# A decoder trunk on one core: the operands' byte addresses, and 1/rms moved from up to down's results

## The chip, the core and the metric

The kernel runs on one of the eight cores of a Trainium2 chip. The metric is the device time of one execution in microseconds (us), as the median of several runs. A profile is one more execution, recorded instruction by instruction. The engines are PE (TensorE, which multiplies matrices; its weight loads are listed as PEld), DVE (VectorE), ACT (ScalarE), POOL (GpSimd) and SP, which here only issues DMAs. They run side by side, each through its own list of instructions in order, and wait for one another by semaphores.

## The reference

The input is a sequence of 512 tokens with 1024 features in float32. There are two layers, and in each one a feed-forward block (FFN), a mixer, and a second FFN, every one of them behind an RMS norm:

```
def rmsnorm(x, g):
    y = x * rsqrt(mean(x * x, axis=-1) + 1e-6)
    return y * g
def swiglu(h, w_gate, w_up, w_down):
    return (silu(h @ w_gate) * (h @ w_up)) @ w_down
x = x + 0.5 * swiglu(rmsnorm(x, g[0]), w_gate[i, 0], w_up[i, 0], w_down[i, 0])
x = x + mixer(rmsnorm(x, g[1]))     # layer 0: attention, layer 1: Mamba-2 SSD
x = x + 0.5 * swiglu(rmsnorm(x, g[2]), w_gate[i, 1], w_up[i, 1], w_down[i, 1])
...
return rmsnorm(x, final_norm)
```

The FFN's hidden width is 2816. The mixer of layer 0 is sliding-window and native sparse attention, that of layer 1 a Mamba-2 scan. The 1/rms of a norm is one number per token, so it can be multiplied in at any place before the next nonlinear step: before silu on the gate, and anywhere down to the result on the up branch.

## The kernel before

Activations lie transposed, features in the 128 partitions and the 512 tokens along the free dimension: `xT` is 8 pieces of 128x512, and `d` counts the pieces. To keep float32 accuracy with the faster float32r matmul, each operand is split into a rounded high part and the rest (`xh` and `xl`, `whi` and `wlo`), and `mm3` (L118 to L122) multiplies high by high, high by low and low by high into the same PSUM bank. A norm's gain is multiplied into `xh` and `xl` when they are made; the 1/rms (`rB`, a PSUM bank of 128x512) is not, and is multiplied into results.

An FFN (`ffn`, L1091) goes twice through the stages gate_up and down, each time with 11 of the 22 tiles of 128 hidden features. In gate_up each tile `f` needs the 128x512 results of gate and up. The first one or two tiles of an FFN are done plainly (`gate_up_direct`, with 512 columns to a matmul): two in the first FFN, one in the others. The other 83 tiles of the program use a Strassen-Winograd scheme (`gate_up`): seven products p1 to p7 with 256 columns each, 84 matmuls in all, whose weights are sums that POOL makes (`sa`, `sb`, L1166). The right-hand operands are the 8 slots of 256 columns in `xh` and `xl`. ACT casts the weights to `whi` (L95), DVE subtracts to get `wlo` (L96), and the two have three buffers each. DVE adds the products up to `gu` (four instructions of L1211), `scale_gu` multiplies gate and up, 1024 columns, by 1/rms (L1219), ACT takes silu of the gate (L1223), DVE multiplies by up (L1224), and `pair` (L240) splits the product to `ah` and `al`, the operands of down. Five PSUM banks (`bs`) serve the products, four of them to a tile.

In down each of the 8 pieces `d` is a sum over the 11 tiles, 33 matmuls with 512 columns on `ah` and `al`, into one of two banks (`bm`). `residual` (L1229) adds half of it to `xT`. In the second half of an FFN the piece then goes to the next norm (`norm_piece`). `last` (L1258) does the same for the very last piece in two halves of 256 columns, with the final norm behind it.

The mixers use `xh` and `xl` with 512 columns: 14 tiles of queries and keys in attention, 48 tiles of the SSM's input (`ssm_tiles`), 24 matmuls each. Later matmuls of attention read probabilities (`th`, `tl`, L548 to L551), those of the SSM's output read `yh` and `yl`.

`xh` and `xl` come from a pool that is filled from the right-hand end of SBUF, and that is opened anew for each norm (`open_x`, L141). In the built program they and the other operands start at these bytes of a partition:

| tile | byte | past a multiple of 128 |
|---|---|---|
| `xh`, `xl` in the FFNs | 163808, 196576 | 96 |
| `xh`, `xl` in the mixers | 196576, 212960 | 96 |
| `ah`, `al` | 78720, 101248 | 0 |
| `th`, `tl` in attention's second part | 195776 to 210112 | 64 |
| `yh`, `yl` | 95104 to 117632 | 0 |
| `whi`, `wlo` | 33664 to 54144 | 0 |

Slots and pieces are 1024 and 2048 bytes long, so every matmul on a tile has the tile's own offset. The order on each engine is not the code's: a scheduler that estimates durations sorts the instructions of every engine when the program is built.

Of the kernel before, what the change touches and what calls it, by code (L numbers as in the profile page):

```python
# [14 lines left out]
F32 = mybir.dt.float32  # L15
# [6 lines left out]
P = 128  # L22
# [18 lines left out]
class Trunk:  # L41
    def __init__(self, ctx, tc, aps):
        self.ctx, self.tc, self.nc, self.aps = ctx, tc, tc.nc, aps
        nc = self.nc
        self.cst = ctx.enter_context(tc.tile_pool(name="cst", bufs=1))
        self.wp = ctx.enter_context(tc.tile_pool(name="wp", bufs=3))
        self.rawp = ctx.enter_context(tc.tile_pool(name="rawp", bufs=2))
        self.one = ctx.enter_context(tc.tile_pool(name="one", bufs=1))
        self.xT = self.cst.tile([P, ND, T], F32, name="xT")
        self.xpool = None  # L50
        self.gains = self.cst.tile([P, 7, ND], F32, name="gains")
        nc.sync.dma_start(out=self.gains, in_=aps["gains"])
        self.epsc = self.cst.tile([P, 1], F32, name="epsc")
        nc.vector.memset(self.epsc, EPS)
        self.onesD = self.cst.tile([P, P], F32, name="onesD")
        nc.vector.memset(self.onesD, 1.0 / D)
        self.n = 0
        self.ahead = None
        nc.scalar.preload_act_table_set("natural_log_exp_and_others")
# [81 lines left out]
    def open_x(self):  # L141
# [9 lines left out]
        shape = [P, 4, 8, 256] if self.strassen else [P, ND, T]  # L151
        self.xh = pool.tile(shape, F32R, name=f"xh_{self.n}")
        self.xl = pool.tile(shape, F32R, name=f"xl_{self.n}")

    def close_x(self):
        if self.xpool is not None:
# [934 lines left out]
    def ffn(self, li, fi, nxt):  # L1091
        nc, tc = self.nc, self.tc
        with tc.tile_pool(name=f"a{li}{fi}", bufs=1, reuse_waits="tile") as ap, tc.tile_pool(
# [9 lines left out]
            for st in range(2):  # L1103
# [5 lines left out]
                for d in DORD:  # L1109
# [9 lines left out]
                            for f in range(k0, k0 + n):  # L1119
                                self.mm3(b, *w[f], ah[:, f], al[:, f], f == 0, f == HF - 1)  # L1120
                    if not end:
                        self.residual(d, b, 0.5, st == 1)
                if self.which == 6 and st == 1:
                    self.last(d, w, ah, al)

# [8 lines left out]
    def gate_up_direct(self, li, fi, f, ah, al):  # L1134
# [8 lines left out]
                self.mm3(b.rearrange("p (i t) -> p i t", i=2), hi[:, d], lo[:, d], *x, d == 0, d == 7)  # L1143
        if f == 0:
            self.late_operands()
        t = self.ft([P, 7, 256], "gu")
        g, u = (t[:, i : i + 2].rearrange("p i t -> p (i t)") for i in (1, 3))
        for out, b in zip((g, u), bs):
            nc.scalar.copy(out=out, in_=b)
        self.scale_gu(t)  # L1150
        self.activate(bs[0], g, u, ah, al)

    def gu_weights(self, li, fi, f, engine):

# [14 lines left out]
    def gate_up(self, li, fi, f, ah, al):  # L1169
# [35 lines left out]
        for out, x, y in (  # L1205
# [3 lines left out]
            (t[:, 2:4], t[:, 0:7:6], halves(bw)),  # L1209
        ):  # L1210
            nc.vector.tensor_tensor(out=out, in0=x, in1=y, op=ALU.add)  # L1211
        self.scale_gu(t)
        g, u = (t[:, i : i + 2].rearrange("p i t -> p (i t)") for i in (1, 3))
        self.activate(by, g, u, ah, al)

    def scale_gu(self, t):
        gu = t[:, 1:5].rearrange("p (m i) t -> p m (i t)", m=2)
        r = self.rB.unsqueeze(1).to_broadcast([P, 2, T])
        self.nc.vector.tensor_tensor(out=gu, in0=gu, in1=r, op=ALU.mult)  # L1219

    def activate(self, b, g, u, ah, al):

        self.nc.scalar.activation(out=b, in_=g, func=AF.Silu)  # L1223
        self.nc.vector.tensor_tensor(out=b, in0=u, in1=b, op=ALU.mult)  # L1224
        self.pair(ah, al, b)

    def residual(self, d, b, scale, last=True, acc=None, ts=slice(0, T)):
        x = self.xT[:, d, ts]
        self.nc.vector.scalar_tensor_tensor(  # L1229
            out=x, in0=b, scalar=scale, in1=x, op0=ALU.mult, op1=ALU.add  # L1230
        )
        if not last:
            return
        if self.which == 6:
            self.square_piece(self.xT[:, d])
        else:
            self.norm_piece(d, acc=acc, late=d % 4 == 3)
# [20 lines left out]
    def last(self, d, w, ah, al):  # L1258
# [9 lines left out]
        for ts, n in zip(halves, (4, 2)):  # L1268
            b = self.bank("m")[:, ts]
            for f in range(HF):  # L1270

                with self.tc.issue_after(mean) if ts.start and f > 3 else nullcontext():
                    self.mm3(b, *w[f], ah[:, f, ts], al[:, f, ts], f == 0, f == HF - 1)
            self.residual(d, b, 0.5, False, ts=ts)
            x = self.xT[:, d, ts]
            ms, r = self.bank("s")[:, ts], self.bank("s")[:, ts]
            sq, y, z = (self.t512(t)[:, ts] for t in ("s", "t1", "t2"))
# [115 lines left out]
```

## Time and profile before

| | us |
|---|---|
| median of 3 runs (2237.49 to 2240.22) | 2237.62 |
| the profiled execution's own time | 2238.98 |
| its span, first to last instruction | 2237.2 |
| PE busy in it | 2167.8 (97%) |
| DVE busy | 1675.6 (75%) |
| ACT busy | 1154.4 (52%) |
| POOL busy | 810.3 (36%) |

The time outside the span is 1.8 us. Matmuls are pipelined: one lasts some 0.28 us with 256 columns and 0.39 us with 512, while the next starts long before it has ended. So the rate of PE is read from starts, not from durations: the start of one matmul and that of a later one, divided by the number of matmuls between. A DVE instruction starts up to 0.08 us before the one in front of it has ended.

### The profile page before, as it was taken

The page shows a single profiled execution, that of the slowest core. Times are in us where ns is not written, and L with a number is a line of the kernel's source. Part 1 is how long each engine was busy: PE and PEld are TensorE (multiplying, and loading weights), DVE is VectorE, ACT ScalarE, POOL GpSimd, SP SyncE. Part 2 cuts the span into 40 slices and gives each one's busy share as a digit, 9 for nine tenths or more (in the row PEclk, how much of TensorE's full clock was granted, in tenths as well). Part 3 has the DMA queues.
Part 4 walks back from the last instruction along what each step waited for, and adds up shares of the span by engine and source line. Part 5 has one row for each costly group of instructions (what it writes and reads, how often), then busy time and mean ns, then how long its engine had stood idle before and what let it go on. Part 6 is the DMA issues. An engine that isn't in the chain of part 4 may idle for free.

```text
span 2237.2 us, 34473 instructions
## 1 busy us (share of the span) xinstructions
PE 2167.8 (97%) x13488; PEld 1935.3 (87%) x13488; DVE 1675.6 (75%) x2430; ACT 1154.4 (52%) x1814; POOL 810.3 (36%) x602
## 2 busy tenths in 40 slices
PE   8999999978999999999999999999999998999998
PEld 5999997867888998998998997788788877998997
DVE  6975984585788975986984984677667668984984
ACT  7533544445566533445542444677667666442543
POOL 1623621432013623622632630244344435622630
PEclk9999999989999999999999999999999999999999
DMA  3222335516302322232322233656565651232322
GB/s 132 95 97 102 107 104 147 133 48 152 76 2 66 114 97 102 96 103 96 112 97 102 95 109 106 172 142 151 118 157 142 160 143 57 104 103 96 114 97 83
DMA packets 48449, 242.04 MB, mean 108 GB/s; under 512 B 6624, under 2 KB 9696, under 8 KB 31136
## 3 DMA queue, kind: packets, MB, share of 16 engines
q1 hardware_dynamic: 36048, 195.28, 25.7%
q0 software_dynamic: 12240, 44.57, 10.5%
q8 instruction: 106, 1.74, 0.3%
q14 instruction: 55, 0.45, 0.1%
HBM read 193.04 MB, written 2.23 MB: 87 GB/s over the span
## 4 chain that ended last, share of the span: by engine, by line
PE 88%; DVE 6%; ACT 2%; DMA 1%; issue 1%; POOL 0%; DVEq 0%; SPq 0%; ACTq 0%; POOLq 0%
PE bm L120 14%; PE bm L122 13%; PE bm L121 13%; PE bs L120 13%; PE bs L122 13%; PE bs L121 13%; DMA wlo<-raw 1%; PE bt L536 1%; DVE xl L244 1%; PE bs L487 1%; DVE wlo L96 1%; PE bo L551 1%; PE bs L482 1%; PE bo L548 1%; PE bs L488 0%
## 5 line engine op out<-in xcount | busy, mean ns | idle before, releaser
L120 PE MATMUL bs<-xh,whi 128*128 128x256 f32 (+1 forms) x2404 | 684.5, 289 | 8.8 <-ACT whi L95 2.9
L121 PE MATMUL bs<-xl,whi 128*128 128x256 f32 (+1 forms) x2404 | 682.0, 286 | 4.1 <-DVE xl L244 4.1
L122 PE MATMUL bs<-xh,wlo 128*128 128x256 f32 (+1 forms) x2404 | 665.5, 287 | 4.5 <-DVE wlo L96 4.5
L95 ACT CAST whi<-raw 128x1024 fp32r<-128x1024 f32 (+3 forms) x312 | 256.8, 826 | 449.4 <-PE bm L121 221.7
L120 PEld LDWEIGHTS bs<-xh,whi 128*128 128x128 f32 x2404 | 452.0, 188 | 25.2 <-issue 9.6
L121 PEld LDWEIGHTS bs<-xl,whi 128*128 128x128 f32 x2404 | 453.4, 189 | 10.8 <-DVE xl L244 5.9
L122 PEld LDWEIGHTS bs<-xh,wlo 128*128 128x128 f32 x2404 | 444.1, 189 | 10.5 <-DVE wlo L96 5.8
L96 DVE TENSOR_TENSOR wlo<-raw,whi 128x1024 fp32r<-128x1024 f32 (+3 forms) x304 | 350.9, 1157 | 111.0 <-ACT whi L95 109.2
L1166 POOL TENSOR_TENSOR sa<-raw 128x512 f32<-128x512 f32 x82 | 111.8, 1364 | 674.2 <-DVE wlo L96 294.5
L121 PE MATMUL bm<-al,whi 128*128 128x512 f32 (+1 forms) x715 | 276.0, 386 | 0.0
L122 PE MATMUL bm<-ah,wlo 128*128 128x512 f32 (+1 forms) x715 | 275.8, 386 | 0.0
L120 PE MATMUL bm<-ah,whi 128*128 128x512 f32 (+1 forms) x715 | 274.8, 386 | 0.0
L109 POOL DMA_DIRECT2D wlo<-raw x85 | 73.6, 866 | 452.6 <-ACT wlo L108 447.2
L1229 DVE SCALAR_TENSOR_TENSOR xT<-bm,xT 128x512 f32<-128x512 f32 (+1 forms) x113 | 77.3, 685 | 165.3 <-PE bm L122 165.3
L122 PE MATMUL bm<-xh,wlo 128*128 128x512 f32 x488 | 195.4, 401 | 4.5 <-DMA wlo<-raw 4.5
L120 PE MATMUL bm<-xh,whi 128*128 128x512 f32 x488 | 195.9, 401 | 1.5 <-DVE xT L1229 0.9
L121 PE MATMUL bm<-xl,whi 128*128 128x512 f32 x488 | 194.5, 399 | 0.0
L1166 POOL TENSOR_TENSOR sa<-sa,raw 128x512 f32<-128x512 f32 x82 | 168.0, 2049 | 5.7
L122 PEld LDWEIGHTS bm<-ah,wlo 128*128 128x128 f32 x715 | 134.3, 188 | 27.1
L121 PEld LDWEIGHTS bm<-al,whi 128*128 128x128 f32 x715 | 134.3, 188 | 26.9
L120 PEld LDWEIGHTS bm<-ah,whi 128*128 128x128 f32 x715 | 134.3, 188 | 26.7
L96 DVE TENSOR_TENSOR wlo<-sb,whi 128x1024 fp32r<-128x1024 f32 x83 | 152.7, 1839 | 1.3 <-ACT whi L95 1.3
(397 smaller groups left out, 4245.2 us busy)
## 6 DMA issues: line engine op xcount, KB each, us to landing
raw<-wgu SPq DMA_DIRECT2D x88, 1024.0 KB
raw<-wdn SPq DMA_DIRECT2D x64, 704.0 KB
wlo<-raw POOLq DMA_DIRECT2D x85, 512.0 KB, 4.7
raw<-m_win SPq DMA_DIRECT2D x24, 1024.0 KB
raw<-m_wout SPq DMA_DIRECT2D x8, 1024.0 KB
raw<-wqk SPq DMA_DIRECT2D x6, 1024.0 KB
raw<-cw SPq DMA_DIRECT2D x4, 1024.0 KB
raw<-wo SPq DMA_DIRECT2D x4, 1024.0 KB
```

Of the source, the lines that this page charges most:

```text
L95: nc.scalar.copy(out=hi[:, :n], in_=raw)
L96: (lo_engine or nc.vector).tensor_tensor(out=lo[:, :n], in0=raw, in1=hi[:, :n].bitcast(F32), op=ALU.subtract)
L109: nc.gpsimd.dma_start(out=lo[:, :n], in_=raw, accum_op=ALU.add)
L120: nc.tensor.matmul(out, wh, xh, start=start, stop=False)
L121: nc.tensor.matmul(out, wh, xl, start=False, stop=False)
L122: nc.tensor.matmul(out, wl, xh, start=False, stop=stop)
L244: nc.vector.tensor_tensor(out=lo, in0=src, in1=hi.bitcast(F32), op=ALU.subtract)
L482: nc.tensor.matmul(s[j], q_hi, k_hi, start=True, stop=False)
L487: nc.tensor.matmul(s[j], q_hi, k_lo, start=False, stop=False)
L536: nc.tensor.transpose(t[:, at : at + P], p[:, j, k0 : k0 + P], self.idf)
L1166: engine.tensor_tensor(out=out, in0=x, in1=y, op=op)
L1229: self.nc.vector.scalar_tensor_tensor(out=x, in0=b, scalar=scale, in1=x, op0=ALU.mult, op1=ALU.add)
```

## The change

Two things change. First, a tile of 32 bytes (`edge`) is put at the right-hand end of SBUF, and in the mixers a tile of 64 bytes (`xe`) beside `xh` and `xl`. That moves the operands:

| tile | byte before | byte now | past a multiple of 128 now |
|---|---|---|---|
| `xh`, `xl` in the FFNs | 163808, 196576 | 163776, 196544 | 64 |
| `xh`, `xl` in the mixers | 196576, 212960 | 196480, 212864 | 0 |

Second, `scale_gu` is gone. The gate alone is multiplied by 1/rms, from `gu` into a PSUM bank (L1225 of the new kernel), and silu works in that bank. In the plain tiles gate is read from its bank without a copy. Up is left as it is; instead `residual` multiplies each result of down by 1/rms, in its bank (L1233), before it is added. For that an SBUF copy of 1/rms, `rF`, is made once for each FFN.

```
+        edge = ctx.enter_context(tc.tile_pool(name="edge", bufs=1, side="right"))
+        edge.tile([P, 8], F32, name="edge")
...
         self.xl = pool.tile(shape, F32R, name=f"xl_{self.n}")
+        if not self.strassen:
+            pool.tile([P, 16], F32, name=f"xe_{self.n}")
...
-                        self.residual(d, b, 0.5, st == 1)
+                        self.residual(d, b, 0.5, st == 1, r=self.rF)
...
-        t = self.ft([P, 7, 256], "gu")
-        g, u = (t[:, i : i + 2].rearrange("p i t -> p (i t)") for i in (1, 3))
-        for out, b in zip((g, u), bs):
-            nc.scalar.copy(out=out, in_=b)
-        self.scale_gu(t)
-        self.activate(bs[0], g, u, ah, al)
+        if f == 0:
+            r = self.rB
+            self.rF = self.ft([P, T], "rF", 1)
+            nc.scalar.copy(out=self.rF, in_=r)
+        u = self.ft([P, 7, 256], "gu")[:, 3:5].rearrange("p i t -> p (i t)")
+        nc.scalar.copy(out=u, in_=bs[1])
+        self.activate(bs[0], bs[0], self.rF, u, ah, al)
...
-        self.scale_gu(t)
         g, u = (t[:, i : i + 2].rearrange("p i t -> p (i t)") for i in (1, 3))
-        self.activate(by, g, u, ah, al)
-
-    def scale_gu(self, t):
-        gu = t[:, 1:5].rearrange("p (m i) t -> p m (i t)", m=2)
-        r = self.rB.unsqueeze(1).to_broadcast([P, 2, T])
-        self.nc.vector.tensor_tensor(out=gu, in0=gu, in1=r, op=ALU.mult)
-
-    def activate(self, b, g, u, ah, al):
-        self.nc.scalar.activation(out=b, in_=g, func=AF.Silu)
+        self.activate(by, g, self.r, u, ah, al)
+
+    def activate(self, b, g, r, u, ah, al):
+        self.nc.vector.tensor_tensor(out=b, in0=g, in1=r, op=ALU.mult)
+        self.nc.scalar.activation(out=b, in_=b, func=AF.Silu)
         self.nc.vector.tensor_tensor(out=b, in0=u, in1=b, op=ALU.mult)
         self.pair(ah, al, b)
 
-    def residual(self, d, b, scale, last=True, acc=None, ts=slice(0, T)):
+    def residual(self, d, b, scale, last=True, acc=None, ts=slice(0, T), r=None):
         x = self.xT[:, d, ts]
+        if r is not None:
+            self.nc.vector.tensor_tensor(out=b, in0=b, in1=r[:, ts], op=ALU.mult)
         self.nc.vector.scalar_tensor_tensor(
             out=x, in0=b, scalar=scale, in1=x, op0=ALU.mult, op1=ALU.add
         )
...
-            self.residual(d, b, 0.5, False, ts=ts)
+            self.residual(d, b, 0.5, False, ts=ts, r=self.rF)
```

The scheduler's order changes with it. The new file's lines stand 3 to 8 further down: L99 is the old L96, L1218 the old L1211, L1227 the old L1224, L249 the old L244. On DVE one tile of gate_up, in the second half of the first FFN, stood as follows (`wlo` belongs to the weights of the tile behind it, `al` to the tile in front).

```order
L1219 TENSOR_TENSOR gu_2692<-gu_2692,br_169 128x1024
L96 TENSOR_TENSOR wlo_2801<-raw_2704,whi_2800 128x512
L1224 TENSOR_TENSOR bs_2601<-gu_2692,bs_2601 128x512
L1211 TENSOR_TENSOR gu_2816<-e_2817,bs_2725 128x2x256
L96 TENSOR_TENSOR wlo_2837<-raw_2828,whi_2836 128x1024
L1211 TENSOR_TENSOR gu_2816<-gu_2816,bs_2726 128x256
L244 TENSOR_TENSOR al_88<-bs_2601,ah_87 128x512
L1211 TENSOR_TENSOR gu_2816<-gu_2816,bs_2724 128x2x256
L96 TENSOR_TENSOR wlo_2841<-sa_2830,whi_2840 128x1024
L1211 TENSOR_TENSOR gu_2816<-gu_2816,bs_2727 128x512
L96 TENSOR_TENSOR wlo_2845<-sb_2831,whi_2844 128x1024
```

The same tile on DVE now:

```order
L1225 TENSOR_TENSOR bs_2613<-gu_2704,br_173 128x512
L99 TENSOR_TENSOR wlo_2813<-raw_2716,whi_2812 128x512
L1227 TENSOR_TENSOR bs_2613<-gu_2704,bs_2613 128x512
L1218 TENSOR_TENSOR gu_2828<-e_2829,bs_2737 128x2x256
L249 TENSOR_TENSOR al_92<-bs_2613,ah_91 128x512
L99 TENSOR_TENSOR wlo_2849<-raw_2840,whi_2848 128x1024
L1218 TENSOR_TENSOR gu_2828<-gu_2828,bs_2738 128x256
L1218 TENSOR_TENSOR gu_2828<-gu_2828,bs_2736 128x2x256
L99 TENSOR_TENSOR wlo_2853<-sa_2842,whi_2852 128x1024
L1218 TENSOR_TENSOR gu_2828<-gu_2828,bs_2739 128x512
L99 TENSOR_TENSOR wlo_2857<-sb_2843,whi_2856 128x1024
```

The multiplication by 1/rms has 512 columns instead of 1024, and `al` has moved from behind the large `wlo<-raw` to the place in front of it. On ACT the same tile stood thus:

```order
L1223 ACTIVATE bs_2601<-gu_2692 128x512
L1204 COPY e_2817<-bs_2724 128x256
L95 CAST whi_2836<-raw_2828 128x1024
L243 CAST ah_87<-bs_2601 128x512
L95 CAST whi_2840<-sa_2830 128x1024
```

And on ACT it stands now (L98 is the old L95, L248 the old L243, L1211 the old L1204):

```order
L1226 ACTIVATE bs_2613<-bs_2613 128x512
L1211 COPY e_2829<-bs_2736 128x256
L248 CAST ah_91<-bs_2613 128x512
L98 CAST whi_2848<-raw_2840 128x1024
L98 CAST whi_2852<-sa_2842 128x1024
```

The cast to `ah` has passed the cast of the next weights to `whi`, as `al` did on DVE. In down of the same half, one piece on DVE was this:

```order
L1229 SCALAR_TENSOR_TENSOR xT<-bm_3355,xT 128x512
L96 TENSOR_TENSOR wlo_3459<-raw_3456,whi_3458 128x768
L223 TENSOR_TENSOR acc_3251<-acc_3251,t_364_3400 128x512
L168 SCALAR_TENSOR_TENSOR xl_3205<-xT,gains,xh_3204 128x512
L96 TENSOR_TENSOR wlo_3481<-raw_3456,whi_3480 128x640
```

And one piece is now:

```order
L1233 TENSOR_TENSOR bm_3371<-bm_3371,rF_288 128x512
L99 TENSOR_TENSOR wlo_3477<-raw_3474,whi_3476 128x768
L1234 SCALAR_TENSOR_TENSOR xT<-bm_3371,xT 128x512
L228 TENSOR_TENSOR acc_3265<-acc_3265,t_365_3417 128x512
L173 SCALAR_TENSOR_TENSOR xl_3217<-xT,gains,xh_3216 128x512
L99 TENSOR_TENSOR wlo_3499<-raw_3474,whi_3498 128x640
```

Each piece has one instruction of 512 columns more, and the first `wlo` stands between the two steps of the residual.

## Rows read from the trace of the kernel before

**Rows 1.** The page: busy time of the engines, and the chain by engine.

```profile
PE 2167.8 (97%) x13488; PEld 1935.3 (87%) x13488; DVE 1675.6 (75%) x2430; ACT 1154.4 (52%) x1814; POOL 810.3 (36%) x602
...
PE 88%; DVE 6%; ACT 2%; DMA 1%; issue 1%; POOL 0%; DVEq 0%; SPq 0%; ACTq 0%; POOLq 0%
```

**Rows 2.** Windows, length, engines' busy time, clock: early tile, late tile, start, down, stage.

```profile
219.08:229.16 10.08, 10.08 (x86) 10.08 (x85) 9.81 (x12) 5.16 (x7) 6.43 (x4) 1.00 0.30 105
280.41:290.80 10.39, 10.31 (x84) 10.13 (x85) 10.32 (x12) 5.07 (x8) 6.42 (x4) 1.00 0.30 100
44.00:58.00 14.00, 9.34 (x64) 7.89 (x63) 13.37 (x23) 9.12 (x15) 3.11 (x2) 1.00 0.22 75
333.00:340.50 7.50, 7.50 (x35) 6.22 (x34) 3.73 (x5) 2.81 (x4) 0.00 (x0) 1.00 0.28 97
198.80:311.30 112.50, 112.11 (x925) 111.14 (x924) 107.81 (x118) 54.56 (x75) 62.54 (x40) 1.00 0.29 98
```

**Rows 3.** Timeline: start us, length us, PE in gate_up, 84 matmuls apart.

```profile
753.39 0.28 PE L120 MATMUL bs<-xh,whi 128*128 128x256 f32 x1
...
763.47 0.28 PE L120 MATMUL bs<-xh,whi 128*128 128x256 f32 x1
```

**Rows 4.** Timeline of PE in down, 33 matmuls apart.

```profile
176.39 0.39 PE L120 MATMUL bm<-ah,whi 128*128 128x512 f32 x1
...
183.87 0.39 PE L120 MATMUL bm<-ah,whi 128*128 128x512 f32 x1
```

**Rows 5.** Timeline of PE in attention's input, 12 matmuls apart.

```profile
395.56 0.39 PE L120 MATMUL bm<-xh,whi 128*128 128x512 f32 x1
...
398.36 0.39 PE L120 MATMUL bm<-xh,whi 128*128 128x512 f32 x1
```

**Rows 6.** Timeline of PE in attention: pairs 4 and 7 matmuls apart.

```profile
591.08 0.28 PE L548 MATMUL bo<-th,vh 128*128 128x256 f32 x1
...
591.53 0.39 PE L551 MATMUL bo<-tl,vh 128*128 128x256 f32 x2
...
609.75 0.28 PE L548 MATMUL bo<-th,vh 128*128 128x256 f32 x1
...
610.58 0.28 PE L549 MATMUL bo<-th,vl 128*128 128x256 f32 x1
```

**Rows 7.** DVE by form in four late tiles: busy us, mean ns, idle before.

```profile
L96 DVE TENSOR_TENSOR wlo<-raw,whi 128x1024 fp32r<-128x1024 f32 x4 | 8.7, 2172 | 0.0
...
L96 DVE TENSOR_TENSOR wlo<-sa,whi 128x1024 fp32r<-128x1024 f32 x4 | 4.9, 1214 | 0.0
L1219 DVE TENSOR_TENSOR gu<-gu,br 128x1024 f32<-128x1024 f32 x4 | 4.8, 1207 | 0.0
...
L1224 DVE TENSOR_TENSOR bs<-gu,bs 128x512 f32<-128x512 f32 x4 | 2.8, 696 | 0.3
```

**Rows 8.** Timeline around the border of two late tiles.

```profile
279.87 0.41 DVE L1211 TENSOR_TENSOR gu<-gu,bs 128x256 f32<-128x256 f32 x1
...
280.06 0.28 PE L122 MATMUL bs<-xh,wlo 128*128 128x256 f32 x1
...
280.42 0.36 PE L120 MATMUL bs<-xh,whi 128*128 128x256 f32 x1
```

**Rows 9.** Timeline of DVE, ACT and POOL inside a late tile.

```profile
287.08 1.05 ACT L95 CAST whi<-raw 128x1024 fp32r<-128x1024 f32 x1
...
287.96 1.28 POOL L1166 TENSOR_TENSOR sb<-raw,sa 128x512 f32<-128x512 f32 x1
288.03 0.58 ACT L243 CAST ah<-bs 128x512 fp32r<-128x512 f32 x1
288.16 2.17 DVE L96 TENSOR_TENSOR wlo<-raw,whi 128x1024 fp32r<-128x1024 f32 x1
```

**Rows 10.** Timeline: attention's first matmul, and the first residual of the tail.

```profile
372.22 0.47 PE L120 MATMUL bm<-xh,whi 128*128 128x512 f32 x1 [0.88 <-DVE xT L1229]
...
2221.80 0.42 DVE L1229 SCALAR_TENSOR_TENSOR xT<-bm,xT 128x256 f32<-128x256 f32 x1 [1.87 <-PE bm L122]
```

## The prediction

> **What bounds the kernel now.** I read the page first: PE is busy for 97% of the span and carries 88% of the chain that ended last, DVE 6% of it [rows 1]. So the time is the sum over PE's matmuls, and where PE waits, it waits mostly for DVE. The windows say in which stage. An early tile of gate_up takes 10.08 us with PE never idle; a late tile of the same stage takes 10.39, with DVE busy for 10.32 of it [rows 2]. The late tile's border shows the wait: DVE's addition starts at 279.87, lasts 0.41, and only then does the next tile's first matmul start, 0.36 after the matmul in front of it, where 0.12 is the normal distance [rows 8]. DVE is thus a little too slow for PE in gate_up, and falls behind until the buffers between them are used up. In down it has half its time free (3.73 of 7.50), and PE never waits [rows 2].
>
> The timeline of PE then gives the pace of a matmul, from start to start. In gate_up, operands 96 bytes past a multiple of 128, 84 matmuls take 10.08 us: 120.0 ns each with 256 columns [rows 3]. In down, operands at multiples of 128, 33 take 7.48: 226.7 ns with 512 columns [rows 4]. In attention's input, operands again 96 past, 12 take 2.80: 233.3 with the same 512 columns [rows 5]. And `th`, 64 past a multiple of 128 and 256 columns, shows two paces: 4 in 0.45 us (113) and 7 in 0.83 (118) [rows 6]. All four have the same instruction form, in full streams of PE, and in gate_up and down the granted clock is 1.00, the upper level of 2.4 GHz [rows 2]; the offset is what differs between the two sorts of 512 columns.
>
> **Gate_up, PE's side.** At 64 past a multiple of 128 the nearest rows are those of `th`: a tile of 84 then takes 84 x 0.113 = 9.5 to 84 x 0.118 = 9.9 us instead of 10.08. The bound below is the change of nothing, 10.08, if `xh` behaves otherwise than `th`; above nothing there is no row, since every pace of 256 columns that was read is 120 or less.
>
> **Gate_up, DVE's side.** The multiplication by 1/rms with 1024 columns (1207 ns) goes, and one with 512 columns comes. Its operands are those of the multiplication by up, one from SBUF and one from PSUM, which takes 696 [rows 7]. So DVE loses 0.51 us per tile, and a late tile that DVE paces takes 10.39 - 0.51 = 9.88 us. That falls within PE's 9.5 to 9.9. I take 9.88 for every tile: DVE then has just what PE's slower pace needs, and no slack is drawn on.
>
> The new order matters to DVE too. `al` passes the large `wlo<-raw`, and on ACT the cast to `ah` passes the cast that this `wlo` waits for. Before, the cast started at 287.08 and lasted 1.05, so `wlo` began at 288.16; it lasted 2.17, as POOL's addition from 287.96 to 289.24 stood against it [rows 9], while the same form on `sa` takes 1.21 [rows 7]. Now `ah` goes first (0.58), `al` runs on DVE in the place of the wait, and `wlo` starts about 1.06 us later, near 289.22: just when POOL has ended. If it then takes 1.21, it ends at 290.43 instead of 290.33, with `al` done already. So about 0.6 us of DVE's queue is won there when POOL keeps its place, and lost when it doesn't. I count neither, since POOL's place shifts with the tile.
>
> How often the border wait of 0.31 us (10.39 - 10.08) occurs before, I take from the length of a whole stage: 11 tiles in 112.50 us, where 11 x 10.08 are 110.88, so 1.62 or five waits, all in its later tiles [rows 2]. The four stages of 11 tiles have 21 of them; the four shorter ones, with 9 or 10 tiles after the plain ones, I put at 10 by the same pattern. That is 31. So 83 x 10.08 + 31 x 0.31 = 846.2 us becomes 83 x 9.88 = 820.0: **-26.2**. The five plain tiles stand where DVE is just as full (13.37 of 14 us at the start, [rows 2]); each loses the same 0.51: **-2.5**.
>
> **Mixers.** 14 + 48 tiles of 24 matmuls are 1488. At a multiple of 128 they should run as `ah` and `al` do: 233.3 - 226.7 = 6.67 ns each, -9.9 us in all [rows 4, 5]. In these stages other matmuls, the norm's and the scores', come between, and a stream that is interrupted doesn't always return to its pace at once; I take **-8.5**, with 0 and -9.9 as its ends.
>
> The Trainium skill, "TensorE: Matmul & The Clock Gate", section "Back-to-back issue gap", knows only columns and a constant: its formula gives 109.2 ns for 256 columns and 215.8 for 512, with no term for the address. This case's trace disagrees, by 120.0 and by the pair 226.7 and 233.3. By that rule the addresses would give nothing, and DVE's relief alone would be left; as a mechanism of this kernel that is the third rival.
>
> **Down.** 64 multiplications of 512 columns in all (the tail's in halves), 0.70 each by the 696 ns [rows 7]. DVE goes from 3.73 to about 4.4 of 7.5 us per piece [rows 2]; what hides them is this free time and the second bank, which gives `residual` a whole piece's 7.48 us to read the first. So **0**. Without this cover, all 64 would cost 45 us. Not covered is the end of an FFN, where the next mixer waits for the last residual: attention's first matmul waited 0.88 for it [rows 10], and now waits for one multiplication more: **+0.7**, and the SSM's input, taken alike, **+0.7**. In the tail `residual` works on halves of 256 columns, 0.42 each [rows 10], and one more for each of two stands on the last chain: **+0.8**. `rF` costs one ACT copy in each FFN, behind the plain tile's matmuls: 0.
>
> **Sum.** -26.2 - 2.5 - 8.5 + 0.7 + 0.7 + 0.8 = -35.0. The profiled execution's own time is 2238.98 (the span of 2237.2 and 1.8 around it, both in the table above), so 2204. The runs' median is 1.4 lower than this execution; the forecast as a median is **2203**.
>
> **Rivals.**
>
> *PE runs ahead* (28%). If `xh` locks to the quicker pace of `th` [rows 6], PE needs 9.5 us for a tile and DVE 9.88. The first tiles of a stage then run at PE's pace until DVE's lead is used up, as they do now. The lead is worth 1.5 us now (five early tiles times 0.31, [rows 2]). It may be up to 2.9, since in the new order a tile's first product goes into a bank that the last additions don't hold, and the bank they do hold is needed only 12 matmuls, some 1.4 us, later. Eight stages give 12 to 23 us more: 2180 to 2191, say 2186. For it: 4 in 0.45 is the longest clean row of `th` alone. Against it: 7 in 0.83 is as clean.
>
> *The FFNs stay at 120* (13%). What holds for `th` need not hold for two operands that alternate. Then 83 tiles take 10.08, only the border waits go (31 x 0.31 = 9.6), and the rest stays: -9.6 - 2.5 - 8.5 + 2.2 = -18.4, about 2220.
>
> *Addresses count for nothing* (7%), and the differences between [rows 3 to 6] come from something else, such as the weights or the bank. Then -9.6 - 2.5 + 2.2 = -9.9: 2228. That the change doesn't do what it says with the addresses ends here too.
>
> *DVE stalls in the new order* (6%, slower). `wlo<-raw` now waits on ACT for `ah` first, which can only be cast after silu and the multiplication by up. If DVE idles there for 0.45 us per tile (`al` at 0.6 filling the rest of 1.06), and POOL's addition then meets the `wlo<-sa` behind it, which goes from 1214 to 2172 ns [rows 7], DVE's tile is 9.88 + 0.45 + 0.96 = 11.29. Before, the mean tile was 846.2 / 83 = 10.20. So 83 x 1.09 = +90.8 - 8.5 = about 2320. It decides once DVE loses more than some 0.4 us per tile: 9.88 + 0.43 is 10.31, and then 83 x 0.11 eats up the mixers' 8.5. For it: DVE has almost no free time in late tiles. Against it: POOL is busy for only 6.4 of 10.4 us [rows 2], and an instruction that starts later because of ACT lets POOL finish first. The Trainium skill, "SBUF — State Buffer", section "Who interferes with whom", says that a DVE instruction with two SBUF inputs contends with a GpSimd instruction that reads SBUF, and that the one which issued first holds on for its whole length. The trace agrees: 2172 against 1214, for the same form, differing in whether POOL is at work. It says nothing on which of the two will be first in the new order.
>
> **How the numbers follow.** The likeliest case is the sum (46%); its own range is 2195 to 2212: down by 8 where DVE's gain of order and half of PE's lead come in, up by 9 where a third of the tiles still waits as now. PE ahead at 2186 is 28%, the FFNs at 120 are 13%, no address effect 7%, the stall 6%. The range of 2177 to 2224 takes in these three cases (with 3 us beyond the lead's far end for a start of DVE's queue that is faster too, and 4 beyond 2220 for the mixers at half their gain) and leaves out the fourth and the stall. A change of 0.2%, 4.5 us, is about what can be told from none. The first three cases (87%) are faster by more. The fourth, at -9.9, splits: 4% faster and 3% within, should the relief come to half of that. Of the stall 5% is slower, and in 1% it is just made good. So: faster 91%, same 4%, slower 5%.
>
> **What will show it.** Right: in gate_up 84 matmuls take 9.5 to 9.9 us, the mixers' 12 take 2.72 instead of 2.80, late tiles show DVE busy for nearly all of 9.9 and few waits at the border, a piece of down still takes 7.48 with DVE at about 4.4, and attention's first matmul waits about 1.6. If tiles run at 9.5 all through a stage, DVE was cheaper than 9.88 and the second case holds. A late tile in which DVE idles before `wlo<-raw`, or `wlo<-sa` at 2.2, proves the stall. Wrong would be a pace of 120.0 or 233.3 still in the records, pieces of down longer than 7.5, or gains at places that I counted as nothing.

## The result, and the profile after

The changed kernel took 2209.88 us (median of 4 runs, 2208.33 to 2213.22), the kernel before 2237.82 in the same session: a ratio of 0.9875, with a 95% interval of 0.9861 to 0.9889. That is 27.9 us less; 2203 had been predicted, with a range of 2177 to 2224. The profiled execution is the longest of the four, 2213.22 with a span of 2211.4, 25.8 below that of before.

The page, as [rows 1]: busy time of the engines, and the chain by engine.

```profile
PE 2139.6 (97%) x13488; PEld 1919.7 (87%) x13488; DVE 1659.7 (75%) x2495; ACT 1157.1 (52%) x1813; POOL 805.4 (36%) x602
...
PE 85%; DVE 8%; ACT 3%; issue 2%; DMA 2%; POOL 0%; SPq 0%; DVEq 0%; ACTq 0%; POOLq 0%
```

PE lost 28.2 us of busy time with the same 13488 matmuls. That isn't all pace: matmuls overlap, so a border wait of 0.3 us hardly shows as idle time, and in the full stage of [rows 2] PE counts as busy for 112.11 of 112.50 us with five such waits in it. Experiments 1 and 2 tell the two apart. DVE lost 15.9, with 65 instructions more. The windows, in the order of [rows 2]: an early tile, a late tile, the start, one piece of down, and the same full stage.

```profile
215.00:224.90 9.90, 9.90 (x86) 9.90 (x85) 9.56 (x12) 5.14 (x8) 6.42 (x4) 1.00 0.29 103
284.30:294.20 9.90, 9.90 (x87) 9.90 (x86) 8.96 (x11) 5.26 (x8) 6.49 (x4) 1.00 0.27 96
44.00:58.00 14.00, 10.56 (x61) 8.69 (x60) 12.68 (x22) 8.46 (x13) 2.97 (x2) 0.88 0.22 75
330.00:337.50 7.50, 7.50 (x35) 6.22 (x34) 4.43 (x6) 2.84 (x5) 0.00 (x0) 1.00 0.30 96
196.18:305.01 108.83, 108.83 (x926) 108.83 (x925) 101.31 (x119) 55.16 (x75) 62.49 (x40) 1.00 0.29 101
```

Early and late tiles now both take 9.90 us, and in the full stage PE is busy for all of its 108.83 us, where [rows 2] had 112.50. The border wait is gone: 108.83 / 924 = 117.8 ns for each matmul, which is the pace inside a tile (below). DVE is busy for 9.56 in the early tile and 8.96 in the late one, so it has room again. A piece of down has 4.43 us of DVE, as forecast. In the window at the start the granted clock is 0.88, so PE was at the lower level of 1.2 GHz for part of it, in a stretch of many waits (busy for 10.56 of 14.00 us); it is 1.00, the upper level of 2.4 GHz, in the others.

The timeline of PE gives the pace: in gate_up, 84 matmuls apart, and in attention's input, 12 apart.

```profile
749.95 0.28 PE L123 MATMUL bs<-xh,whi 128*128 128x256 f32 x1
...
759.84 0.28 PE L123 MATMUL bs<-xh,whi 128*128 128x256 f32 x1
```

```profile
388.74 0.39 PE L123 MATMUL bm<-xh,whi 128*128 128x512 f32 x1
...
391.46 0.39 PE L123 MATMUL bm<-xh,whi 128*128 128x512 f32 x1
```

9.89 / 84 = 117.8 ns, after 120.0 in [rows 3]; and 2.72 / 12 = 226.7 ns, after 233.3 in [rows 5], the pace that down had in [rows 4]. DVE by form in four late tiles, as [rows 7]:

```profile
L99 DVE TENSOR_TENSOR wlo<-raw,whi 128x1024 fp32r<-128x1024 f32 x4 | 6.0, 1508 | 0.8 <-ACT whi L98 0.8
L99 DVE TENSOR_TENSOR wlo<-sa,whi 128x1024 fp32r<-128x1024 f32 x4 | 4.9, 1218 | 0.0
L99 DVE TENSOR_TENSOR wlo<-raw,whi 128x512 fp32r<-128x512 f32 x4 | 4.0, 1006 | 0.1
...
L1225 DVE TENSOR_TENSOR bs<-gu,br 128x512 f32<-128x512 f32 x4 | 2.7, 685 | 0.0
L1227 DVE TENSOR_TENSOR bs<-gu,bs 128x512 f32<-128x512 f32 x4 | 2.7, 685 | 0.1
```

The multiplication by 1/rms costs 685 ns instead of 1207, and the large `wlo<-raw` now misses POOL's addition in three of these four tiles: 1508 ns on average instead of 2172, 1.29 us where it misses it. Half of that is given back by the small `wlo<-raw`, 1006 now, which in the view of [rows 7] was

```profile
L96 DVE TENSOR_TENSOR wlo<-raw,whi 128x512 fp32r<-128x512 f32 x4 | 2.7, 680 | 0.0
```

Two places lost time. Attention's first matmul waits 1.61 us instead of 0.88 [rows 10]:

```profile
366.65 0.47 PE L123 MATMUL bm<-xh,whi 128*128 128x512 f32 x1 [1.61 <-DVE xT L1234]
```

And on DVE in the tail, the two output multiplications of the first half (L1290, 2.34 us together) stand between the two steps of the last residual:

```profile
2198.27 0.43 DVE L1233 TENSOR_TENSOR bm<-bm,rF 128x256 f32<-128x256 f32 x1 [0.21 <-PE bm L125]
2198.61 2.34 DVE L1290 TENSOR_TENSOR xT<-xT,bs 128x1024 f32<-128x1024 f32 x2
2200.87 0.41 DVE L1234 SCALAR_TENSOR_TENSOR xT<-bm,xT 128x256 f32<-128x256 f32 x1
```

By stages, from the first matmul of one to that of the next (us, the two profiled executions):

| stage | before | after | difference |
|---|---|---|---|
| gate_up, four halves with plain tiles | 484.6 | 475.1 | -9.4 |
| gate_up, four halves of 11 tiles | 449.3 | 435.3 | -13.9 |
| down to attention | 60.9 | 61.65 | +0.8 |
| attention | 322.5 | 319.8 | -2.7 |
| down to the SSM, and the SSM | 537.9 | 534.6 | -3.3 |
| last down and tail | 71.9 | 74.5 | +2.6 |
| other down stages | 59.85 each | 59.87 each | 0 |

### The profile page after: what moved, and what is told of

It reads as the page before. It is cut to its first block, busy times and chain, and to the rows that moved or that the text cites. A ratio compares the mean times of both kernels' runs of the same rounds, so it can differ in the third digit from the quotient of the medians.

```text
span 2211.4 us, 34462 instructions
## 1 busy us (share of the span) xinstructions
PE 2139.6 (97%) x13488; PEld 1919.7 (87%) x13488; DVE 1659.7 (75%) x2495; ACT 1157.1 (52%) x1813; POOL 805.4 (36%) x602
## 4 chain that ended last, share of the span: by engine, by line
PE 85%; DVE 8%; ACT 3%; issue 2%; DMA 2%; POOL 0%; SPq 0%; DVEq 0%; ACTq 0%; POOLq 0%
PE bm L123 13%; PE bm L125 13%; PE bm L124 13%; PE bs L123 13%; PE bs L125 12%; PE bs L124 12%; DMA wlo<-raw 1%; PE bt L541 1%; DVE wlo L99 1%; DVE xl L249 1%; PE bs L492 1%; PE bo L556 1%; PE bs L487 1%; PE bo L553 1%; PE bs L493 0%
## 5 line engine op out<-in xcount | busy, mean ns | idle before, releaser
L98 ACT CAST whi<-raw 128x1024 fp32r<-128x1024 f32 (+3 forms) x312 | 257.0, 827 | 403.5 <-PE bm L124 188.1
L99 DVE TENSOR_TENSOR wlo<-raw,whi 128x1024 fp32r<-128x1024 f32 (+3 forms) x304 | 332.2, 1093 | 91.3 <-ACT whi L98 89.8
L99 DVE TENSOR_TENSOR wlo<-sb,whi 128x1024 fp32r<-128x1024 f32 x83 | 150.8, 1817 | 0.0
L1218 DVE TENSOR_TENSOR gu<-gu,bs 128x512 f32<-128x512 f32 (+1 forms) x249 | 147.4, 592 | 2.7
```

Source lines behind the costliest of these rows:

```text
L98: nc.scalar.copy(out=hi[:, :n], in_=raw)
L99: (lo_engine or nc.vector).tensor_tensor(out=lo[:, :n], in0=raw, in1=hi[:, :n].bitcast(F32), op=ALU.subtract)
```

## The experiments

All were compared with the kernel before on the same chip. A time with a ratio is the median of several runs; the others are single runs, read by the stages of their profile. "Distance", from experiment 6 on, is the byte address of the moving operand minus that of the weights.

**1. Addresses alone.** The kernel before with both pads and nothing else.

```
+        edge.tile([P, 8], F32, name="edge")
...
+        if not self.strassen:
+            pool.tile([P, 16], F32, name=f"xe_{self.n}")
```

> The kernel before with the operands moved alone (1/rms as before). Theory (address and relief of DVE are needed together): a matmul of gate_up could start every 117.9 ns, but DVE still needs 10.3 to 10.4 us for a late tile, so a full stage stays within 1 us of 112.5 (waits at the border of more tiles, about 0.5 us each), and most of what is gained comes from the mixers, 5 to 8 us: about 2228 to 2232. Rival (the addresses alone give the gain): stages of 108.8 and about 2210. Rival (DVE alone): no change, 2237.

It took 2228.80 us, ratio 0.9963 (0.9949 to 0.9976): the theory's number. The same full stage, and the border of two of its late tiles:

```profile
198.80:310.72 111.92, 109.74 (x926) 108.53 (x925) 107.86 (x118) 54.32 (x75) 62.61 (x40) 1.00 0.29 98
```

```profile
277.63 2.18 DVE L98 TENSOR_TENSOR wlo<-raw,whi 128x1024 fp32r<-128x1024 f32 x1
...
279.73 0.41 DVE L1215 TENSOR_TENSOR gu<-gu,bs 128x256 f32<-128x256 f32 x1
279.75 0.28 PE L124 MATMUL bs<-xh,wlo 128*128 128x256 f32 x1
...
280.29 0.36 PE L122 MATMUL bs<-xh,whi 128*128 128x256 f32 x1 [0.27 <-DVE gu L1215]
...
300.17 0.28 PE L124 MATMUL bs<-xh,wlo 128*128 128x256 f32 x1
301.09 0.35 PE L122 MATMUL bs<-xh,whi 128*128 128x256 f32 x1 [0.64 <-DVE gu L1215]
```

Matmuls start 117.8 ns apart, and from the fourth tile on the border takes some 0.54 us where 0.12 is normal; PE is busy for 2.4 us less in the stage, and the stage is as long as before but for 0.6. What PE gains it waits away, since DVE's tile is still 10.4. The tile from 290.69 on shows it best: PE runs at 113.3 there, the border takes 0.92 (last two lines), and the tile 10.40 as the others do. The eight gate_up stages together are 0.1 us shorter. Attention gains 2.7, and the hand-over and the SSM 5.9: 8.6 against the -8.5 of the sum.

**2. 1/rms alone.** The changed kernel without the two pads.

```
-        edge.tile([P, 8], F32, name="edge")
...
-        if not self.strassen:
-            pool.tile([P, 16], F32, name=f"xe_{self.n}")
```

> The changed kernel with the operands back at 96 bytes past a multiple of 128 (both pads left out); the order on the engines is the changed kernel's. Theory (both needed): matmuls of gate_up start every 120.0 ns and the border waits are gone, so a full stage takes 84 x 11 x 0.120 = 110.9 us against 112.5 before and 108.8 in the changed kernel; all eight stages give about -10, the tail and the start of the SSM cost their +5 all the same: about 2230 to 2234. Rival (DVE's relief gives the gain, addresses nothing): 108.8 and 2210. Rival (only addresses count): 2237 or more.

It took 2232.99 us, ratio 0.9979 (0.9969 to 0.9990), and the full stage has no wait left:

```profile
197.40:308.28 110.88, 110.88 (x926) 110.88 (x925) 101.35 (x119) 55.68 (x75) 61.87 (x40) 1.00 0.29 99
```

That is 924 matmuls at 120.0 ns to the last digit. All gate_up stages gain 8.1, and the SSM and the tail lose as in the changed kernel. So the two parts are worth 9.1 and 5.0 alone and 27.9 together; half of the gain appears only with both. That the whole gain is one part's is refuted for both parts.

**3. FFN operands at a multiple of 128.** A pad of 96 bytes, none in the mixers.

```
-        edge.tile([P, 8], F32, name="edge")
+        edge.tile([P, 24], F32, name="edge")
...
-            pool.tile([P, 16], F32, name=f"xe_{self.n}")
```

> The changed kernel with a pad of 96 bytes in place of 32 and none in the mixers: all operands xh and xl at multiples of 128, FFN and mixers. Theory (256 columns want an odd multiple of 64, and 120.0 is their pace at a multiple of 128, as ah with 256 columns showed in the tail): gate_up at 120.0, a full stage 110.9, about 2224 to 2228. Rival (any multiple of 64 will do): 117.9, 108.8 and about 2210.

It took 2226.64 us, ratio 0.9950 (0.9935 to 0.9964).

```profile
197.13:308.00 110.87, 110.87 (x926) 110.87 (x925) 102.19 (x119) 55.56 (x75) 62.38 (x40) 1.00 0.29 99
```

120.0 ns again: what is best for 512 columns is no better than 96 bytes past for 256 columns.

**4. Mixers at 64.** Only the pad of the mixers is left out.

```
-        if not self.strassen:
-            pool.tile([P, 16], F32, name=f"xe_{self.n}")
```

> The changed kernel without the pad of the mixers: their operands at odd multiples of 64 too, the FFNs as in the changed kernel. Theory (512 columns want a multiple of 128): the mixers' matmuls go back from 226.7 to about 231 ns, 3 to 7 us more: 2213 to 2217. Rival (64 is enough for any width): 226.7 and no change, 2210.

It took 2210.09 us, ratio 0.9880 (0.9863 to 0.9898), the changed kernel's time. The pace in attention's input, 18 matmuls apart, is between the two:

```profile
389.15 0.39 PE L123 MATMUL bm<-xh,whi 128*128 128x512 f32 x1
...
393.27 0.39 PE L123 MATMUL bm<-xh,whi 128*128 128x512 f32 x1
```

4.12 / 18 = 228.9 ns. 2.2 ns for each of 1488 matmuls are 3.3 us, which a comparison of medians doesn't show. That is half of the theory's rise to 231, and the mixers' own pad was worth little.

**5. The tail's order, and the SSM's norm asked for earlier.** In the tail, the output multiplications of the first half are queued behind the last residual; in the SSM one line asks for 1/rms ahead of the small product.

```
+                with self.tc.issue_after(add) if not ts.start else nullcontext():
...
+        self.rB
         b = self.bank("m")
         for k in range(ND):
```

> The changed kernel with two places of order mended: in the tail the last residual's two steps stand together, ahead of the output multiplications of the first half, and the SSM's norm matmul is asked for before the matmuls of its first small product. Theory (the 2.6 us that the tail lost and the 5.0 that the SSM lost are due to these orders, not to the added multiplication itself): the tail goes from 74.5 to about 72.4 (0.43 of multiplication stays), the SSM loses at least the wait of 3.5 us for its first gate, from 474.1 to about 470: together 5 to 6 us, about 2204. Rival (DVE and ACT have no room there whatever the order): no change, 2210.

It took 2208.94 us, ratio 0.9866 (0.9843 to 0.9889), not to be told from the changed kernel as a whole. By stages it can be told: last down and tail take 72.43, 2.1 less, with DVE now in this order.

```profile
2199.36 0.43 DVE L1234 TENSOR_TENSOR bm<-bm,rF 128x256 f32<-128x256 f32 x1 [0.21 <-PE bm L125]
2199.83 0.42 DVE L1235 SCALAR_TENSOR_TENSOR xT<-bm,xT 128x256 f32<-128x256 f32 x1
2200.17 2.34 DVE L1297 TENSOR_TENSOR xT<-xT,bs 128x1024 f32<-128x1024 f32 x2
```

So in the tail the order cost 2.1 and the multiplication 0.5. The SSM gained nothing (477.1): its norm matmul came 2 us earlier, but the next step on ACT still stood behind a cast that waited for weights. PE waited 4.5 us for the SSM's first gate (3.5 in the changed kernel), and behind this wait it ran for 5.1 us at a granted clock of 0.50, the lower level; in the changed kernel for 2.2 us. The two stretches, this kernel's first:

```profile
1401.20:1406.30 5.10, 5.10 (x13) 3.97 (x12) 4.96 (x12) 1.40 (x3) 1.28 (x1) 0.50 0.53 126
```

```profile
1402.00:1404.20 2.20, 2.20 (x6) 1.67 (x6) 2.13 (x4) 0.88 (x2) 2.15 (x2) 0.50 0.45 88
```

So such a wait costs more than its own length: the matmuls behind it start 0.43 us apart, against 0.23 at the upper level.

**6. Weights at odd multiples of 64.** Pads on both sides of the weights' pool; the operands of the FFNs and mixers stay where they are (`ah`, `al`, `yh` and `yl` move by 128).

```
+        wpad.tile([P, 16], F32, name="wpad")
         self.wp = ctx.enter_context(tc.tile_pool(name="wp", bufs=3))
+        rpad.tile([P, 16], F32, name="rpad")
```

> The changed kernel with the weights whi and wlo at odd multiples of 64 bytes (before: at multiples of 128), all else as it was. Theory (the moving operand's address alone sets the pace): gate_up stays at 117.9 ns, down at 226.7, 2210. Rival (moving operand and weights get in each other's way, so that the offset between them counts, which would also explain why 256 columns and 512 columns like different offsets): gate_up changes to 113 or 120 ns, that is 2175 or 2226 for the whole.

It took 2242.59 us, ratio 1.0027 (1.0015 to 1.0038): everything that the addresses had brought is gone, and more. The full stage, and down 33 matmuls apart:

```profile
198.25:309.13 110.88, 110.88 (x926) 110.88 (x925) 102.16 (x119) 55.43 (x75) 62.29 (x40) 1.00 0.29 99
```

```profile
159.74 0.40 PE L127 MATMUL bm<-ah,whi 128*128 128x512 f32 x1
...
167.44 0.40 PE L127 MATMUL bm<-ah,whi 128*128 128x512 f32 x1
```

Gate_up is back at 120.0 ns with `xh` where the changed kernel has it, and down is at 7.70 / 33 = 233.3, with `ah` still at a multiple of 128. The theory, which had the operand's own address decide, is refuted. Nor do the new weights' addresses slow everything: the plain tiles, with 512 columns on the same `xh`, gain. Here and in the changed kernel, 18 matmuls apart:

```profile
1050.59 0.39 PE L127 MATMUL bs<-xh,whi 128*128 128x512 f32 x1
...
1054.67 0.39 PE L127 MATMUL bs<-xh,whi 128*128 128x512 f32 x1
```

```profile
1035.64 0.39 PE L123 MATMUL bs<-xh,whi 128*128 128x512 f32 x1
...
1039.76 0.39 PE L123 MATMUL bs<-xh,whi 128*128 128x512 f32 x1
```

That is 226.7 ns at the distance 0, as elsewhere at 0, against 228.9 at 64. What counts is how the operand lies to the weights that PE loads beside it; the distance orders most of what follows, but not all: at 64 the SSM's output runs at 229 here and down at 233.3.

**7. xl apart from xh.** A pad of 64 bytes between them in the FFNs, so that two of three matmuls have the distance 0 modulo 128 and one has 64.

```
+        if self.strassen:
+            pool.tile([P, 16], F32, name=f"xm_{self.n}")
```

> The changed kernel with a pad between xh and xl in the FFNs: xl at an odd multiple of 64, xh at a multiple of 128. Theory (each matmul has the pace of its own operand): two of three matmuls at 120.0 and one at 117.9, mean 119.3, a full stage 110.2. Rival (the pace comes from the step between the two operands' addresses): not between 117.9 and 120.0, 113 or above 120.

A single run: 2221.35 us, and the full stage is 110.09, for which the theory had 110.2:

```profile
196.20:306.29 110.09, 110.09 (x926) 110.09 (x925) 101.50 (x119) 55.59 (x75) 62.35 (x40) 1.00 0.29 100
```

The mean is that of the single paces, (2 x 120.0 + 117.8) / 3 = 119.3, or 110.2 for the stage. Which matmul of the three has which pace the starts don't settle.

**8. Without the multiplication of the gate.**

```
-        self.nc.vector.tensor_tensor(out=b, in0=g, in1=r, op=ALU.mult)
-        self.nc.scalar.activation(out=b, in_=b, func=AF.Silu)
+        self.nc.scalar.activation(out=b, in_=g, func=AF.Silu)
```

> The changed kernel without the multiplication of the gate by 1/rms in all tiles of gate_up (it is left out, so the output isn't the reference's): DVE has 0.69 us less for each tile. Theory (PE's 117.9 ns set the tile of 9.90 us, DVE no longer does): full stages stay at 108.8 us. The prediction's view (DVE sets the tile at 9.88): full stages fall towards 84 x 11 x 0.113 = 104.7.

A single run: 2218.18 us, the full stage 108.83 as in the changed kernel.

```profile
196.42:305.25 108.83, 108.83 (x925) 108.82 (x924) 101.68 (x109) 56.15 (x75) 62.48 (x40) 1.00 0.29 101
```

The stage didn't move, but DVE's busy time didn't fall either (101.68 with ten instructions fewer, 101.31 with them): the large `wlo<-raw` met POOL again and took 2102 ns. So this run doesn't show by itself that DVE has stopped to matter; the last one does.

**9. The SSM's norm first.** As 5, with the small product's matmuls queued behind the norm's.

```
+            with self.tc.issue_after(self.norm_mm) if k >= 0 else nullcontext():
+                self.mm3(b[0:32], wh[:, k], wl[:, k], self.xh[:, k], self.xl[:, k], k == 0, k == ND - 1)
```

> The changed kernel with the tail's order mended, and in the SSM the norm's matmul ahead of the whole first small product, so that 1/rms doesn't wait behind later weights on ACT. Theory (the SSM loses about 5 us because 1/rms is late by some 10 us): the wait of 3.5 to 4.5 us for the first gate goes, the wait for the sum of squares at the hand-over (2.5 us before, some 3 now) comes back; hand-over and SSM together 532 to 534 us, where the changed kernel has 534.6 and its repetitions 536 to 538; with a tail of 72.4 about 2204. Rival (what varies there is the arrival of weights and not this order): 2209.

It took 2212.20 us, ratio 0.9886 (0.9869 to 0.9902): no gain. PE's waits from there to the end of the SSM (us in total, times, longest) in this kernel, and in the changed one:

```profile
PE bs L138 <- DVE acc L228: 4.4, 1, 4.4
PE bs L930 <- DMA lrow<-acs: 4.0, 1, 4.0
```

```profile
PE bm L123 <- DVE t L858: 3.5, 1, 3.5
...
PE bt L787 <- DVE s L784: 1.6, 1, 1.6
```

The waits for L858 and L784 are gone, and in their place 4.4 us are lost at the hand-over and 4.0 to a DMA: hand-over and SSM together are 540.2, longer than the 534.6 of the changed kernel. The wait was turned into others. Something else was to be seen in the first half of the first FFN, where five tiles in a row ran at the quicker pace of `th` [rows 6], without a wait (47.60 us for 5 x 84 matmuls, 113.3 ns each):

```profile
64.73:112.33 47.60, 47.60 (x423) 47.60 (x421) 46.14 (x54) 25.82 (x35) 33.13 (x21) 1.00 0.31 106
```

So DVE did what a tile needs in 9.52 us there, and was busy for 46.14 of the 47.60.

**10. A distance of 32.** A pad of 64 bytes and none in the mixers.

```
-        edge.tile([P, 8], F32, name="edge")
+        edge.tile([P, 16], F32, name="edge")
...
-            pool.tile([P, 16], F32, name=f"xe_{self.n}")
```

> The changed kernel with a pad of 64 bytes and none in the mixers: all operands xh and xl 32 bytes past a multiple of 128, the weights at multiples of 128. Theory (the distance to the weights counts, and anything off 64 costs a piece of a line more): as at 96, gate_up 120.0 and a full stage 110.9, mixers 233 to 235. Rival (smaller distances are cheaper): below 117.9.

A single run: 2211.49 us. The theory is wrong for 256 columns and right for 512: the mixers are at 233.3, but the full stage is the shortest so far.

```profile
192.64:300.44 107.80, 107.80 (x926) 107.80 (x924) 101.14 (x119) 55.02 (x75) 62.30 (x40) 1.00 0.29 102
```

107.80 / 924 = 116.7 ns.

**11. Another 128 bytes.** `edge` with 160 bytes: distances of 192 and 128 modulo 256, in place of 64 and 0.

```
-        edge.tile([P, 8], F32, name="edge")
+        edge.tile([P, 40], F32, name="edge")
```

> The changed kernel with 128 bytes more of pad: the distance of the operands from the weights stays 64 (FFNs) and 0 (mixers) modulo 128, but changes by 128 modulo 256. Theory (only the distance modulo 128 counts): 117.9, full stages 108.8, mixers 226.7 in steady runs. Rival (modulo 256 or more counts): another pace, with 113.3, half of 226.7, as the best to be had.

A single run: 2216.67 us. Full stages take 108.83 as before, so for 256 columns the theory holds there; but the mixers fall back to about 232 ns, so for 512 columns modulo 128 isn't enough. And in one half with a plain tile PE ran at 113.3 ns for most of a tile, and then waited in every tile at the same place:

```profile
754.17 0.28 PE L124 MATMUL bs<-xl,whi 128*128 128x256 f32 x1
754.53 0.38 PE L125 MATMUL bs<-xh,wlo 128*128 128x256 f32 x1
...
764.07 0.28 PE L124 MATMUL bs<-xl,whi 128*128 128x256 f32 x1
764.43 0.39 PE L125 MATMUL bs<-xh,wlo 128*128 128x256 f32 x1
```

```profile
743.20:753.10 9.90, 9.81 (x86) 9.61 (x86) 9.55 (x11) 5.03 (x9) 6.41 (x5) 1.00 0.31 107
```

0.36 us pass there from one start to the next, and the place comes back after 9.90 us: the matmul is the first to need `wlo<-raw`. So in this half DVE and ACT give a tile every 9.90 us, which is also what PE needs at 117.8; why the two agree isn't shown. It is no fixed need of theirs: experiment 9 has 9.52 and experiment 10 has 107.80 / 11 = 9.80, both without a wait.

**12. The best of these.** The FFNs at a distance of 32, the mixers as in the changed kernel, and the tail's order of experiment 5.

```
-        edge.tile([P, 8], F32, name="edge")
+        edge.tile([P, 16], F32, name="edge")
...
-            pool.tile([P, 16], F32, name=f"xe_{self.n}")
+            pool.tile([P, 8], F32, name=f"xe_{self.n}")
```

> The changed kernel with the operands of the FFNs 32 bytes from the weights modulo 128 instead of 64 (a pad of 64 bytes at the edge, one of 32 in the mixers, so that the mixers stay where the changed kernel has them), and the tail's order mended. Theory (116.7 ns at 32, seen in one look, holds; the mixers keep 226.7; the tail loses no 2.1): eight stages of some 107.8 instead of 108.8, and 72.4 in the tail, together -10 against the changed kernel: 2198 to 2202. Rival (the pace at 64 and 32 is a matter of the run, and the gain of the look was luck): 2206 to 2210.

It took 2202.61 us (2198.60 to 2208.46, 5 runs), ratio 0.9844 (0.9824 to 0.9865): some 7 us below the changed kernel and 0.6 above what the theory expected. By stages it came: full stages are 107.80 again, all of gate_up is 8.2 shorter than in the changed kernel's profiled execution, and last down and tail take 72.42, 2.1 less.

```profile
193.30:301.10 107.80, 107.80 (x925) 107.76 (x924) 101.10 (x119) 55.02 (x75) 62.36 (x40) 1.00 0.30 102
```

107.80 / 924 is again 116.7 ns, so PE never waits in this stage either, with the same work for DVE. So in the changed kernel, at 108.83, it is PE's pace that sets the full stages.

## Why the prediction was right, and where it was not

The time, 2209.88, lies in the likeliest case's own range of 2195 to 2212. Its gain of 35 was too large by 7.

- **What bounds the kernel: right.** DVE paced the late tiles. Experiments 1 and 2 show it from both sides: a quicker PE alone moves the stages by nothing, a relieved DVE alone ends the waits and leaves 120.0 ns.
- **The tile of 9.88: the number right, the engine not.** All tiles of the full halves measure 9.90. But PE is never idle and DVE is: it is PE's pace of 117.8, the slower one of `th` [rows 6], that sets them. The working had named it as the other end of the same value. That DVE would need 9.88 too isn't borne out: it took 9.90 where PE was quicker in experiment 11, but kept up at 9.80 (experiment 12) and 9.52 (experiment 9). So that the number came out is partly luck. The four full halves gave -13.9. The sum had -15.3 for them (44 x 0.20 + 21 x 0.31); it took all four to be like the one that it read, and the last took only 111.75 us.
- **The plain tiles and the first halves: too large.** This is the step that failed most. The relief of DVE in these four halves (ten border waits and five plain tiles) was put at 5.6 us; experiment 2, which has that relief alone, shows 2.4. The border waits are not what is missing: the last seven tiles of the four halves, where they lie, give 4.4 us in experiment 2, more than the 3.1 of the sum. The front of these halves, the plain tiles and the first Strassen-Winograd tiles behind them, was to give 2.5 and lost 2.0 instead; in the changed kernel, with the quicker pace, it takes 198.0 us against 197.8 before, so nothing came of it at all. DVE is as full there as the working says, but PE waits there mainly for `xh`, `xl` and the first `wlo` of the FFN's start, not for the multiplication by 1/rms, and in the changed order it waits longer for them: in the second FFN 0.69 us for `wlo`, where it was 0.43, and 0.48 for ACT's `xh`, which is new. All of gate_up gave -23.3 against -28.7.
- **The mixers: right in the pace.** 226.7 for 233.3 came as forecast, and -8.6 against -8.5 in experiment 1, where the order is that of before. The last digit is luck: in the eight executions with these addresses attention takes from 315.4 to 319.8 us, and the granted clock over a stage differs too (attention: 0.94 before, 0.95 in experiment 1, 0.97 in experiment 9, the shortest; hand-over and SSM: 0.99 before, 1.00 in experiment 1). How much of the 8.6 is that, the runs don't tell. The reason behind the pace, the operand's own address, was wrong (experiment 6).
- **Down: right.** 59.87 for eight pieces, with 4.43 us of DVE in a piece.
- **Hand-overs: one right, one not.** Attention paid 0.76 for 0.7. At the SSM 0.7 was forecast; there the scheduler moved the norm's matmul behind 48 others, which saved 2.5 us at the hand-over and cost some 5 in the SSM: 3.5 of waiting for its first gate, and the stretch at the lower clock behind it (experiment 5). The SSM and its hand-over take 532.1 with the addresses alone (experiment 1) and 534.6 with both, 2.5 more; without the addresses it is 537.9 and 540.5 (experiment 2), 2.5 too. How much of that is the order stays open: in the runs with the changed order and the mixers at a distance of 0 or 64 it varies from 534.6 to 538.0, and experiment 9, which put the matmul first, was no better.
- **The tail: wrong by its order.** 0.8 was forecast, 2.6 measured; experiment 5 gives 2.1 to the output multiplications that got between the two steps. The prediction counted the instruction that was added and not what the scheduler would put behind it, though the order shows it.

With the measured terms the sum is -23.3 - 8.6 + 0.8 + 2.5 + 2.6 = -26.0, against -25.8 between the two profiled executions.

Of the rivals, "PE runs ahead" (113.3) did occur, in one half of experiment 9, in parts of experiments 1, 4, 5 and 11, and in one tile of the changed kernel's last FFN (9.54 us, from 1918.70 on), but not in its full stages. "DVE stalls" did not come: the large `wlo<-raw` waits 0.2 us a tile for ACT, and wins 0.66 from POOL, of which the small one loses 0.33. That addresses count for nothing is refuted by experiment 6, which changes nothing but addresses and loses 32.7 us against the changed kernel. There the Trainium skill's formula ("TensorE: Matmul & The Clock Gate", section "Back-to-back issue gap") has no term to tell the two apart. The Trainium skill gives that formula there for the isolated gap of one matmul and not for a stream, which the prediction left out.

## What to carry to other kernels

Two limits that lie 3% apart hide each other: ease both, and try each alone only to see which waits go. Where matmuls follow each other without a gap, measure the pace from start to start, and try the distance between the moving operand and the weights as a parameter; a pad of some bytes is the whole edit. After any edit look at what a scheduler has put between two steps of a short chain, above all at the end of the program.

## What the hardware showed that was not expected

The pace of a matmul depends on how its operand and its weights lie to each other in a partition. Read in the traces by the distance, float32r, weights 128x128, full streams at a granted clock of 1.00:

| distance modulo 256 | 256 columns, ns | 512 columns, ns |
|---|---|---|
| 0 | 120.0 | 226.7 |
| 32 | 116.7 | 233.3 |
| 64 | 117.8, at times 113.3 | 228.9 in mixers and plain tiles, 233.3 in down |
| 96 | 120.0 | 233.3 |
| 128 | not run | some 232 |
| 192 | 117.8, at times 113.3 | 233 |

Of these distances none is best for both widths. 113.3 is half of 226.7. At distances of 64 and 192 a stream can hold either of two paces for many tiles with the same addresses, and goes from one to the other at a wait, in experiment 9 at one of 0.04 us; what selects it, and why the same distance of 64 gives 228.9 in one place and 233.3 in another, stays open. That the distance counts, and not either address by itself, is borne out best at 0, where two different pairs of addresses give the same paces (experiments 3 and 6); at 64 it doesn't settle the pace alone. The rows for 128 and 192 rest on the single run of experiment 11, and for 512 columns at 192 also on the mixers of experiment 6.
